# Weight sums of the second feed-forward: two of four made by accumulating transfers, with the signs of the scheme turned

## The chip, the cores and the metric

The kernel runs on one NeuronCore of a Trainium2 chip. The core has five engines with in-order queues of their own: PE (TensorE, matmuls, with its weight loads shown apart as PEld), DVE (VectorE), ACT (ScalarE), POOL (GpSimd) and SP (SyncE, which here only issues DMAs). They work at the same time and wait for each other through semaphores. Sixteen DMA engines move data between the chip's memory (HBM) and the on-chip memory (SBUF); matmul results go to PSUM banks. The metric is the device time of one execution in microseconds (us); the number of record before the change is the median of three runs.

## The reference, cut to what matters

Two layers of a diffusion backbone work on 512 latent tokens of width 1024 (and 256 context tokens). The part that changes is the feed-forward of the second layer, on the latent tokens alone:

```python
def swiglu(h, w_in, w_out):
    gate, up = jnp.split(h @ w_in, 2, axis=-1)
    return (jax.nn.silu(gate) * up) @ w_out

x = x + mx[5] * swiglu(modulate(rms_norm(x, norm2_g[i]), mx[3], mx[4]), ffn_w_in[i], ffn_w_out[i])
```

The inner width is 2816, that is 22 tiles of 128. A tile needs 128 columns of gate weights and 128 columns of up weights, each 1024 deep. All data is 32-bit.

## The kernel before, in words

The weights lie in HBM as one stream `wst` of chunks of 128 x 1024 (512 KB), in the order of their use; SP loads them through `w_raw`. For each FFN tile there are two chunks: `g` (gate) and `u` (up). Their left 512 columns belong to the first half of the model width, their right 512 to the second.

Precision is kept by splitting each operand into a high and a low part, so that one product is three matmuls (high x high, low x high, high x low). The high part is a cast on ACT (line 164, tile `whi`), the low part a subtraction on DVE (line 165, tile `wlo`); both stand in `split`.

Tiles 0, 1 and 2 of the 22 are computed plainly. Tiles 3 to 21 (19 tiles) go through `seven()`: as in Strassen's method the 2 x 2 block product (two halves of the model width, gate and up, two halves of the tokens) is made with seven block products in place of eight. Each product is twelve matmuls of 256 columns (line 897). This needs sums of token blocks, made once (`token_sums`, split into the tiles `sA`), and sums of weight blocks for every tile, made on DVE by `quarter_sums`, lines 903 to 906, each of 128 x 512. With g and u for the left halves g1, u1 and the right halves g2, u2:

- line 903: g1 becomes u1 - g1
- line 904: u1 becomes u2 - u1
- line 905: u2 becomes u2 - (new g1)
- line 906: g2 becomes g2 - (new u2)

Before these sums the old `g` is split whole into `b11`, and the right half of `u` into `b22` (tile `hm`). After them `u` is split into `b32` and `g` into `b14`. The weight pairs b11, b14 and b32 rotate through a ring of six buffers, so a tile's weights can be made while two tiles before it are still multiplied. `g` has two raw buffers of its own in the pool `fp`; `u` shares two raw buffers in the pool `rp` with the weights of the output.

The products go to PSUM tiles X, Y and Z with two banks each. ACT copies four of them to SBUF (lines 1742, 1744, 1746, 1751), DVE adds where two products meet (lines 1748, 1753, 1755), ACT takes the silu (line 107), and DVE multiplies (line 1757). The activation is split in turn (lines 1768, 1770).

The tiles come in groups of 2, 4, 4, 4, 4 and 4. After the first tile of a group the previous group is multiplied by `w_out` (`output`): eight products into the two PSUM banks of `pj`, each added to the residual by DVE (line 256). So PE does four tiles of `seven()`, then an output, and so on.

The order of instructions on each engine is not that of the text: the framework's planner picks it by its own costs and due times, the order of SP's loads included. `after(instruction, others)` adds an order on one engine without a semaphore. POOL has almost nothing to do in this stage. An accumulating DMA, one that adds its source to what stands in its target, is used twice in the kernel before, in the retention layer (line 1466), and is issued from POOL.

Of the kernel before, what the change touches and what calls it, by code (L numbers as in the profile page):

```python
# [30 lines left out]
HALVES = (slice(0, 256), slice(256, 512))  # L31
# [18 lines left out]
def dit_kernel(ctx, tc, xT, cT, crow, small, consts, masks, tabs0, tabs1, jtab, adaQ, adaN, adaT, wst, out):  # L50
    nc = tc.nc
    mult, add, sub = ALU.mult, ALU.add, ALU.subtract
# [9 lines left out]
    def T(pool, cols, tag, bufs, dt=F32):  # L62
        return pool.tile([P, cols], dt, tag=tag, bufs=bufs, name=tag)
# [27 lines left out]
    def after(ins, others):  # L91
        for o in others:
            tc.add_manual_dep(ins.ins, o.ins.name, order, reason="table set turn")
# [24 lines left out]
    wpos, wsel, ring = [0], [0], []  # L118

    def w_raw(pool=None, bufs=2):  # L120
        raw = T(pool or rp, 1024, "wraw", bufs)
        nc.sync.dma_start(raw, wst[wpos[0]])
        wpos[0] += 1
        return raw

    def w_parts(pool, own=2):

        bufs = own
        if ring:
            pool, bufs = ring[wsel[0] % len(ring)], 2  # L130
        elif wsel[0] % (2 + own) < 2:
            pool, bufs = rp, 2
        wsel[0] += 1
        return T(pool, 1024, "whi", bufs, F32R), T(pool, 1024, "wlo", bufs, F32R)
# [28 lines left out]
    def split(t, hi, lo, behind=()):  # L163
        after(nc.scalar.copy(hi, t), behind)  # L164
        return nc.vector.tensor_tensor(lo, t, hi, op=sub)  # L165
# [19 lines left out]
    def t_sq(n):  # L185
        return T(rp, 512, "sq", 2)[:, :n]

    def t_hn(n):
        return T(rp, 512, "hn", 2)[:, :n]
# [609 lines left out]
    t1 = cp.tile([P, 8], F32, name="lg_t1")  # L799
    t2 = cp.tile([P, 8], F32, name="lg_t2")  # L800
# [90 lines left out]
    def product(o, a, b, c0, first):  # L891

        for k in range(4):
            ws = slice(c0 + k * P, c0 + (k + 1) * P)
            (whi, wlo), (xhi, xlo) = (t[:, ws] for t in b), a(k)
            for i, (p, r) in enumerate(((whi, xhi), (wlo, xhi), (whi, xlo))):
                nc.tensor.matmul(o, p, r, start=first and k + i == 0, stop=k == 3 and i == 2,  # L897
                                 skip_group_check=not first)

    def quarter_sums(g, u, behind=()):  # L900

        l_, r_ = slice(0, 512), slice(512, 1024)
        after(nc.vector.tensor_tensor(g[:, l_], u[:, l_], g[:, l_], op=sub), behind)
        nc.vector.tensor_tensor(u[:, l_], u[:, r_], u[:, l_], op=sub)
        nc.vector.tensor_tensor(u[:, r_], u[:, r_], g[:, l_], op=sub)
        nc.vector.tensor_tensor(g[:, r_], g[:, r_], u[:, r_], op=sub)

    for s in range(2):
        fold_gain(0, s, 1)
    F = ExitStack()  # L910
# [40 lines left out]
    def token_sums():  # L951

        h1, h2 = THIRDS
        for k in range(4):
            t1, t2 = tm[k], tm[k + 4]
            for j in (k, k + 4):
                nc.scalar.activation(tm[j][:, h1], tm[j][:, h1], AF.Identity, bias=mods[0, 0][:, 3, j:j + 1])
            nc.vector.tensor_tensor(t2[:, h2], t1[:, h2], t2[:, h2], op=add)
            nc.vector.tensor_tensor(t1[:, h2], t1[:, h1], t1[:, h2], op=sub)
            nc.vector.tensor_tensor(t1[:, h1], t2[:, h2], t1[:, h1], op=sub)  # L960
            nc.vector.tensor_tensor(park[:, k * 384:(k + 1) * 384], t2[:, h1], t1[:, h1], op=sub)
            for n, t in ((1, t2[:, h2]), (3, t1[:, h2]), (2, t1[:, h1])):
                S[n, k] = parts(quarter())
                split(t, *S[n, k])
# [237 lines left out]
    def chunk(i, own=False):  # L1202
        raw = T(qw, 1024, "wx", 4) if own else T(rp, 1024, "wraw", 2)
        nc.sync.dma_start(raw, wst[i])
        return raw
# [6 lines left out]
    last_split, rope_end, rope_sum, hm, other_sums = [None], [None], [None], [], []  # L1212
# [9 lines left out]
            return lambda k: first(4 * (n[1] == "2") + k, int(n[0]) - 1)  # L1222
        return of

    def token_sums(hm, part, sh2, sums, behind=()):

        q1, q2 = HALVES
        shift = mods[1, 0][:, part]
        nc.vector.tensor_tensor(sh2[:, 0:4], shift[:, 0:4], shift[:, 4:8], op=add)
        for k in range(4):  # L1230
            t1, t2 = hm[k], hm[k + 4]
            after(nc.vector.scalar_tensor_tensor(t2[:, q2], t1[:, q2], sh2[:, k:k + 1], t2[:, q2], add, add), behind)
            nc.vector.tensor_tensor(t1[:, q2], t1[:, q1], t1[:, q2], op=sub)
            nc.vector.scalar_tensor_tensor(t1[:, q1], t2[:, q2], shift[:, k:k + 1], t1[:, q1], sub, sub)
            mid = split(t1, *sums[2 * k + 1])
            nc.vector.scalar_tensor_tensor(t2[:, q1], t2[:, q1], shift[:, k + 4:k + 5], t1[:, q1], add, sub)
            other_sums.append((t2, *sums[2 * k]))
        return mid

    def other_parts():  # L1240
        while other_sums:
            split(*other_sums.pop(0))
# [119 lines left out]
    for hd in range(RH):  # L1362
# [20 lines left out]
        if hd == 0:  # L1383
            sums = token_sums(hm, 0, T(qp, 16, "sh2", 1), h_sum, [normed])
            dx, dcx = strips(0, [sums])
# [149 lines left out]
        for i in range(2):  # L1535
            g, v = chunk(bg + i), chunk(bv + i)
# [101 lines left out]
        def first_weights(room, behind=()):  # L1638
            raw = w_raw()
            hi, lo = room()  # L1640
            ahead.append((hi, lo))
            after(nc.scalar.copy(hi, raw), behind)
            return nc.vector.tensor_tensor(lo, raw, hi, op=sub)
# [3 lines left out]
        hm = [T(hM, 512, "hm", 8) for _ in range(KT)]  # L1647
# [26 lines left out]
        for i in (5, 7):  # L1674
            weights_end = first_weights(hW_parts, done[i:i + 1])

    norm_end, first_end, first_mult, first_adds = [], [], [], []
# [15 lines left out]
    sh2 = T(fp, 48, "sh2", 1)  # L1693
    sA = [(T(fp, 512, "sA", 16, F32R), T(fp, 512, "sA", 16, F32R)) for _ in range(KT)]
# [32 lines left out]
    def seven(late=()):  # L1727
        g, u = w_raw(fp, 2), w_raw()
        b11 = w_parts(fp, 4)
        b22 = T(hM, 512, "hm", 8, F32R), T(hM, 512, "hm", 8, F32R)  # L1730
        b14, b32 = w_parts(fp, 4), w_parts(fp, 4)
        split(g, *b11, norm_end)
        split(u[:, 512:1024], *b22, norm_end)
        quarter_sums(g, u, first_end[1:2])
        split(u, *b32, first_adds)
        after(split(g, *b14, first_adds), late)
        X, Y, Z = (T(psF, 512, n, 2)[:, 0:SC] for n in "XYZ")
        t, up = t_hn(SX), t_sq(SX)
        e1, e2 = T(rp, 512, "res", 12), T(rp, 512, "res", 12)
        p1, z1, u2, u3 = e1[:, HALVES[0]], e1[:, HALVES[1]], e2[:, HALVES[0]], e2[:, HALVES[1]]  # L1740
        product(Y, operand_a("11"), b11, 0, True)
        act_parts([nc.scalar.copy(p1, Y)])
        product(Z, operand_a(1), b14, 0, True)
        copies[:] = [nc.scalar.copy(z1, Z)]
        product(Y, operand_a(2), b32, 512, False)
        copies.append(nc.scalar.copy(u2, Y))  # L1746
        product(X, operand_a("12"), b11, 512, True)
        nc.vector.tensor_tensor(t[:, HALVES[0]], p1, X, op=add)
        silu(t[:, HALVES[0]], t[:, HALVES[0]])
        product(Y, operand_a(3), b32, 0, False)  # L1750
        nc.scalar.copy(u3, Y)
        product(Z, operand_a(4), b22, 0, False)
        nc.vector.tensor_tensor(up[:, HALVES[0]], u2, Z, op=add)
        product(Y, operand_a("22"), b14, 512, False)
        nc.vector.tensor_tensor(up[:, HALVES[1]], u3, z1, op=add)
        silu(t[:, HALVES[1]], Y)
        nc.vector.tensor_tensor(t, t, up, op=mult)
        act = new_act()
        pending.append((t, *act))
        return act  # L1760
# [3 lines left out]
    def act_parts(behind=()):  # L1764
        ends = []
        while pending:
            t, hi, lo = pending.pop()
            ends.append(nc.scalar.copy(hi, t))
            after(ends[0], behind)
            ends.append(nc.vector.tensor_tensor(lo, t, hi, op=sub))  # L1770
        return ends
# [24 lines left out]
    for gsz in FFN_GROUPS:  # L1796
        acts = []
        for i in range(gsz):
            if f < 2:
                acts.append(first[f])  # L1800
            elif f == 2:
                w = [next_w(fp, behind=norm_end) for _ in range(2)]
                token_sums(hm, 3, sh2, sA, [weights_end])
                other_parts()
                acts.append(plain(w))
            else:
                acts.append(seven(late))
            late = output(prev, False) if i == 0 and prev is not None else ()
            f += 1
        prev = acts  # L1810
# [146 lines left out]
```

## Time and profile before

| what | value |
|---|---|
| median of 3 runs | 1734.41 us (1733.25 to 1735.33) |
| the profiled execution | 1732.25 us, of which the span of the profile 1730.3 us |
| granted TensorE clock | 0.999 |
| PE busy | 1698.0 us, 98% of the span |
| DVE busy | 1361.0 us, 79% |
| ACT busy | 871.1 us, 50% |
| POOL busy | 50.5 us, 3% |
| first line 903 to last line 906 | 1420.2 us to 1686.5 us |

How to read the rows: in a list of groups, `L164 ACT CAST whi<-wraw` is the line, the engine, the operation, and what it writes and reads; `x19` is a count. In a list of waits, `A <- B: total, times, longest` says that A's engine sat idle until B was done. In the timeline the columns are the start, the duration, and the instruction, with the idle time before it in brackets. In a table of stretches each engine has its busy time and its number of instructions. DMA rows give the size of one transfer in KB and the median time from issue to landing.

### The profile page before, as it was taken

The page shows a single profiled execution, that of the slowest core. Times are in us where ns is not written, and L with a number is a line of the kernel's source. Part 1 is how long each engine was busy: PE and PEld are TensorE (multiplying, and loading weights), DVE is VectorE, ACT ScalarE, POOL GpSimd, SP SyncE. Part 2 cuts the span into 40 slices and gives each one's busy share as a digit, 9 for nine tenths or more (in the row PEclk, how much of TensorE's full clock was granted, in tenths as well). Part 3 has the DMA queues.
Part 4 walks back from the last instruction along what each step waited for, and adds up shares of the span by engine and source line. Part 5 has one row for each costly group of instructions (what it writes and reads, how often), then busy time and mean ns, then how long its engine had stood idle before and what let it go on. Part 6 is the DMA issues. An engine that isn't in the chain of part 4 may idle for free.

```text
span 1730.3 us, 27786 instructions
## 1 busy us (share of the span) xinstructions
PE 1698.0 (98%) x10876; PEld 1513.0 (87%) x10876; DVE 1361.0 (79%) x2436; ACT 871.1 (50%) x1552; POOL 50.5 (3%) x168
## 2 busy tenths in 40 slices
PE   7999999999999999999999999999999999999999
PEld 5788877899999999999988788898897899899998
DVE  6698889798778788787889858858758798877874
ACT  5587779465433334342556534524525464445442
POOL 0000000000000000000000000000000000000000
PEclk9999999999999999999999999999999999999999
DMA  9612221543253434343423524523423223333322
GB/s 349 239 30 57 62 62 56 209 134 121 73 157 117 153 110 148 123 154 102 156 99 88 183 77 132 163 82 124 159 90 108 95 74 103 117 102 116 100 86 86
DMA packets 62803, 207.48 MB, mean 120 GB/s; under 512 B 7248, under 2 KB 8912, under 8 KB 62416
## 3 DMA queue, kind: packets, MB, share of 16 engines
q1 hardware_dynamic: 55184, 178.97, 32.0%
q0 software_dynamic: 7200, 26.22, 5.2%
q8 instruction: 85, 1.39, 0.3%
q10 hardware_dynamic: 288, 0.52, 0.1%
q14 instruction: 46, 0.38, 0.1%
HBM read 199.65 MB, written 2.10 MB: 117 GB/s over the span
## 4 chain that ended last, share of the span: by engine, by line
PE 78%; DVE 11%; DMA 6%; ACT 3%; issue 2%; SPq 0%; ACTq 0%; DVEq 0%
PE Y L897 14%; PE pj L147 7%; PE Z L897 7%; PE pj L149 7%; PE pj L148 7%; PE Z L1292 6%; PE X L897 3%; DMA wraw<-in_wst_dram 3%; PE pT L736 2%; PE pO L750 2%; PE S L710 2%; DVE wlo L165 2%; PE Y L1281 2%; PE pj L1292 2%; PE X L1281 1%
## 5 line engine op out<-in xcount | busy, mean ns | idle before, releaser
L164 ACT CAST whi<-wraw 128x1024 fp32r<-128x1024 f32 x258 | 270.0, 1051 | 333.7 <-PE Z L149 81.9
L165 DVE TENSOR_TENSOR wlo<-wraw,whi 128x1024 fp32r<-128x1024 f32 x258 | 314.3, 1221 | 64.5 <-ACT whi L164 62.7
L897 PE MATMUL Y<-aq,whi 128*128 128x384 f32 x640 | 173.5, 335 | 0.6 <-ACT hn L1053 0.6
L897 PEld LDWEIGHTS Y<-aq,whi 128*128 128x128 f32 x640 | 116.6, 188 | 1.6 <-ACT hn L1053 1.4
L256 DVE SCALAR_TENSOR_TENSOR res<-pj,mod,res 128x512 f32<-128x512 f32 (+1 forms) x112 | 81.0, 728 | 41.5 <-PE pj L149 41.2
L897 PE MATMUL Y<-aq,wlo 128*128 128x384 f32 x320 | 107.0, 334 | 0.0
L273 DVE CUSTOM_DVE_ANT_0 y<-adaw,crow,small_sb 128x1024 bf16<-128x1024 f32 x64 | 81.9, 1280 | 29.6 <-DMA adaw<-in_adaT_dram 29.4
L1292 PE MATMUL Z<-whi,sA 128*128 128x512 f32 x256 | 81.7, 394 | 1.4 <-ACT gate L1478 1.4
L101 ACT ACTIVATE pr<-pr,stat,qs 128x513 f32<-128x513 f32 (+2 forms) x96 | 74.2, 775 | 9.1 <-DVE stat L717 8.8
L147 PE MATMUL pj<-ax,whi 128*128 128x512 f32 x176 | 69.0, 392 | 1.2 <-DVE res L256 1.2
L149 PE MATMUL pj<-ax,whi 128*128 128x512 f32 x176 | 68.6, 390 | 0.0
L148 PE MATMUL pj<-ax,wlo 128*128 128x512 f32 x176 | 68.6, 390 | 0.0
L147 PE MATMUL pj<-act,whi 128*128 128x512 f32 x168 | 65.6, 391 | 0.0
L148 PE MATMUL pj<-act,wlo 128*128 128x512 f32 x168 | 65.5, 390 | 0.0
L149 PE MATMUL pj<-act,whi 128*128 128x512 f32 x168 | 65.5, 391 | 0.0
L897 PEld LDWEIGHTS Y<-aq,wlo 128*128 128x128 f32 x320 | 60.1, 188 | 0.0
L1292 PEld LDWEIGHTS Z<-whi,sA 128*128 128x128 f32 x256 | 48.0, 188 | 13.0 <-ACT gate L1478 2.6
L711 DVE CUSTOM_DVE_ANT_0 pr<-S,mask,qs 128x256 f32<-128x256 f32 (+1 forms) x96 | 53.1, 566 | 7.8 <-PE S L710 5.3
L897 PE MATMUL Y<-sA,whi 128*128 128x256 f32 x304 | 58.1, 277 | 0.6 <-ACT res L1746 0.6
L897 PE MATMUL Y<-hx,whi 128*128 128x256 f32 x304 | 56.3, 277 | 0.0
L736 PE MATMUL pT<-const_sb,pr 128*128 128x128 f32 x352 | 53.6, 278 | 1.5 <-ACT tt L738 0.9
L1292 PE MATMUL Z<-wlo,sA 128*128 128x512 f32 x128 | 50.7, 396 | 0.2
(581 smaller groups left out, 5070.4 us busy)
## 6 DMA issues: line engine op xcount, KB each, us to landing
wraw<-in_wst_dram SPq DMA_DIRECT2D x224, 512.0 KB, 3.6
adaw<-in_adaT_dram POOLq DMA_DIRECT2D x48, 512.0 KB, 3.9
wx<-in_wst_dram SPq DMA_DIRECT2D x30, 512.0 KB, 4.3
adan<-in_adaQ_dram SPq DMA_DIRECT2D x16, 512.0 KB, 8.8
adan<-in_adaN_dram SPq DMA_DIRECT2D x12, 512.0 KB, 7.7
adaw<-in_adaT_dram SPq DMA_DIRECT2D x8, 512.0 KB, 3.9
res<-in_xT_dram SPq DMA_DIRECT2D x14, 256.0 KB, 3.2
aq<-in_adaN_dram SPq DMA_DIRECT2D x12, 256.0 KB, 5.7
```

The costliest lines, as they stand in the source:

```text
L101: ins = nc.scalar.activation(*args, **kw)
L147: nc.tensor.matmul(o, whi, xhi, start=first, stop=False)
L148: nc.tensor.matmul(o, wlo, xhi, start=False, stop=False)
L149: return nc.tensor.matmul(o, whi, xlo, start=False, stop=last)
L164: after(nc.scalar.copy(hi, t), behind)
L165: return nc.vector.tensor_tensor(lo, t, hi, op=sub)
L256: return nc.vector.scalar_tensor_tensor(res[d], o, mods[l, s][:, part, d:d + 1], res[d], mult, add)
L273: res.append(nc.vector.tensor_tensor_reduce(junk, w, cr[:, s * 1024:(s + 1) * 1024], 1.0, sm_t[:, C_ADAB + l * 48 + j:C_ADAB + l * 48 + j ...
L711: nc.vector.tensor_tensor_reduce(pt[:, c0:c0 + w], bank, mask[:, m0:m0 + w], 1.0, top, add, ALU.min, lo)
L736: nc.tensor.transpose(tp[:, a * P:(a + 1) * P], self.pr[(0, 2, 1, 3)[a]][:, ki * P:(ki + 1) * P], ident)
L897: nc.tensor.matmul(o, p, r, start=first and k + i == 0, stop=k == 3 and i == 2, skip_group_check=not first)
L1292: ins = nc.tensor.matmul(os[t], p, r, start=first and k + i == 0, stop=k == 3 and i == 2, skip_group_check=by_k or not first)
```

## The change

In the second feed-forward's `seven()` the four weight sums are replaced by sums without a minus, and the first two of them are made by DMAs that POOL issues and that add to their target in SBUF:

- u1 becomes u1 + u2: an accumulating transfer of 128 x 512 (256 KB) that reads the right half of the same chunk of `wst` from HBM again
- g1 becomes g1 + u1: a second one that reads the left half of u's chunk from HBM
- u2 becomes u2 + (new g1): on DVE, as before, with an addition
- g2 becomes g2 + (new u2): on DVE, as before, with an addition

The second transfer reads `wst`, not the tile `u`, so it doesn't depend on u's load; it does depend on the split of `g` into `b11`, which reads g1 first. To make up for the signs, the token sums swap an addition with a subtraction, and the two sums that form `up` become differences. `token_sums` gets the two operators as an argument; the call in the retention layer keeps the old ones.

```diff
-    def quarter_sums(g, u, behind=()):
-
-        l_, r_ = slice(0, 512), slice(512, 1024)
-        after(nc.vector.tensor_tensor(g[:, l_], u[:, l_], g[:, l_], op=sub), behind)
-        nc.vector.tensor_tensor(u[:, l_], u[:, r_], u[:, l_], op=sub)
-        nc.vector.tensor_tensor(u[:, r_], u[:, r_], g[:, l_], op=sub)
-        nc.vector.tensor_tensor(g[:, r_], g[:, r_], u[:, r_], op=sub)
...
-    def token_sums(hm, part, sh2, sums, behind=()):
+    def token_sums(hm, part, sh2, sums, behind=(), ops=(add, sub)):
...
-        nc.vector.tensor_tensor(sh2[:, 0:4], shift[:, 0:4], shift[:, 4:8], op=add)
+        plus, minus = ops
+        nc.vector.tensor_tensor(sh2[:, 0:4], shift[:, 0:4], shift[:, 4:8], op=plus)
...
-            after(nc.vector.scalar_tensor_tensor(t2[:, q2], t1[:, q2], sh2[:, k:k + 1], t2[:, q2], add, add), behind)
+            after(nc.vector.scalar_tensor_tensor(t2[:, q2], t1[:, q2], sh2[:, k:k + 1], t2[:, q2], add, plus), behind)
...
-            nc.vector.scalar_tensor_tensor(t2[:, q1], t2[:, q1], shift[:, k + 4:k + 5], t1[:, q1], add, sub)
+            nc.vector.scalar_tensor_tensor(t2[:, q1], t2[:, q1], shift[:, k + 4:k + 5], t1[:, q1], add, minus)
...
         split(g, *b11, norm_end)
-        split(u[:, 512:1024], *b22, norm_end)
-        quarter_sums(g, u, first_end[1:2])
+        l_, r_ = slice(0, 512), slice(512, 1024)
+        nc.gpsimd.dma_start(u[:, l_], wst[wpos[0] - 1][:, r_], accum_op=add)
+        split(u[:, r_], *b22, norm_end)
+        nc.gpsimd.dma_start(g[:, l_], wst[wpos[0] - 1][:, l_], accum_op=add)
+        after(nc.vector.tensor_tensor(u[:, r_], u[:, r_], g[:, l_], op=add), first_end[1:2])
+        nc.vector.tensor_tensor(g[:, r_], g[:, r_], u[:, r_], op=add)
         split(u, *b32, first_adds)
         after(split(g, *b14, first_adds), late)
...
-        nc.vector.tensor_tensor(up[:, HALVES[0]], u2, Z, op=add)
+        nc.vector.tensor_tensor(up[:, HALVES[0]], Z, u2, op=sub)
...
-        nc.vector.tensor_tensor(up[:, HALVES[1]], u3, z1, op=add)
+        nc.vector.tensor_tensor(up[:, HALVES[1]], z1, u3, op=sub)
...
-                token_sums(hm, 3, sh2, sA, [weights_end])
+                token_sums(hm, 3, sh2, sA, [weights_end], (sub, add))
```

## The prediction

> **What bounds the kernel now.** I read the engine sums of the page first, then stretches of 50 us over the second feed-forward, because the share of a whole span says little about one stage.
>
> ```profile
> PE 1698.0 (98%) x10876; PEld 1513.0 (87%) x10876; DVE 1361.0 (79%) x2436; ACT 871.1 (50%) x1552; POOL 50.5 (3%) x168
> ```
>
> ```profile
> 1400.00:1450.00 50.00, 48.47 (x370) 45.93 (x370) 48.13 (x75) 27.84 (x45) 0.00 (x0) 1.00 0.27 85
> 1450.00:1500.00 50.00, 49.74 (x338) 45.14 (x337) 37.87 (x53) 22.29 (x38) 0.00 (x0) 1.00 0.40 120
> 1500.00:1550.00 50.00, 50.00 (x371) 47.17 (x370) 38.45 (x54) 24.68 (x43) 0.00 (x0) 1.00 0.33 103
> ...
> 1650.00:1700.00 50.00, 50.00 (x347) 46.25 (x346) 37.33 (x51) 22.86 (x37) 0.00 (x0) 1.00 0.27 85
> ```
>
> The columns after the stretch's length are PE, PEld, DVE, ACT and POOL busy, the granted clock (1.00) and the DMA share. From 1500 us PE has no idle time at all while DVE rests a quarter of the time; only in the first stretch is DVE nearly full (48.13 of 50) and PE idle (1.53 us). Next the waits between 1415 us and the end, as us in total, times, longest:
>
> ```profile
> ACT whi L164 <- DVE wraw L905: 23.3, 18, 2.7
> ...
> PEld pj L147 <- DVE res L256: 2.0, 2, 1.4
> PE pj L147 <- DVE res L256: 1.2, 2, 1.0
> ...
> PEld Y L897 <- ACT res L1746: 0.8, 1, 0.8
> PE Y L897 <- ACT res L1746: 0.6, 1, 0.6
> ```
>
> PE's three waits (2.0 + 0.8 = 2.8 us by the weight loads, 1.2 + 0.6 = 1.8 us by the matmuls) are all that PE loses to DVE and ACT over the 19 tiles that change. ACT does wait for the weight sums (23.3 us), but that is an engine with half its time free.
>
> **What the change removes.** Lines 903 and 904 go; 905 and 906 stay as additions.
>
> ```profile
> L903 DVE TENSOR_TENSOR wraw<-wraw x19: 677/683/694, 1420.2 to 1683.6; 128x512 f32<-128x512 f32 x19
> ```
>
> ```profile
> L904 DVE TENSOR_TENSOR wraw<-wraw x19: 676/683/685, 1421.7 to 1684.5; 128x512 f32<-128x512 f32 x19
> ```
>
> 2 x 19 x 0.683 = 26.0 us of DVE busy time. What covers it is PE, full in every stretch after 1500 us, so there it is worth nothing; it can be worth at most the 2.8 us above, in the early stretch. The turned signs (token sums, lines 1753 and 1755) change operators, not counts or shapes: nothing, since the same instruction stands in the same place.
>
> **What it adds.** 38 accumulating transfers of 256 KB (38 x 256 KB = 10.0 MB more read from HBM), issued from POOL. This kernel already has two of twice the size, at line 1466:
>
> ```profile
> wraw<-in_wst_dram SPq DMA_DIRECT2D x224, 512.0 KB, 3.6
> adaw<-in_adaT_dram POOLq DMA_DIRECT2D x48, 512.0 KB, 3.9
> out_dram<-res SPq DMA_DIRECT2D x8, 256.0 KB, 2.0
> wraw<-in_wst_dram POOLq DMA_DIRECT2D x2, 512.0 KB, 5.7
> ```
>
> ```profile
> L1466 POOL DMA_DIRECT2D wraw<-in_wst_dram x2: 861/872/884, 934.4 to 939.0; - x2
> ...
> DMA to landing us min/median/max: 5.3/5.7/6.1
> ```
>
> The DMA view of 930 to 950 us holds those two and about as many plain bytes, so it prices the engines' time (last column: share of 16 engines):
>
> ```profile
> q0 software_dynamic: 288, 1.05, 32.3%
> q1 hardware_dynamic: 260, 1.01, 15.4%
> ```
>
> An accumulated byte takes twice a plain one: 32.3% of 20 us is 6.5 us on each engine for two transfers, 3.2 us each. Half the size saves half of that, 1.6 us, so I take **T = 5.7 - 1.6 = 4.1 us** from issue to landing. Bounds: 2.0 us (a plain 256 KB store) and 6.1 us (the slower 512 KB accumulate, as if the size saved nothing). 4.1 is nearest the accumulating row, the only one of its kind. The Trainium skill, page "DMA: Bandwidth & Descriptors", section "Anatomy of one DMA — SWDGE (gpsimd) path", fits 2.0 us + bytes/436e3 for a transfer issued from GpSimd, an estimate of 2.6 us for 256 KB and 3.2 us for 512 KB. The row of 512 KB says 5.7 us where the accumulate is done, so here the row decides; with 2.6 us the case below would have 2.5 us to spare instead of 1.0 and the total would be the same.
>
> Engine time added: 38 x 1.6 = 61 us on each DMA engine over some 310 us, which lifts the share from about 0.3 to 0.5; a weight load that meets one lands up to 1.6 us later. POOL issues 38 x 0.87 = 33 us and has nothing else in these stretches (0.00 busy).
>
> **The waits that it adds.** The transfer into u's left half waits for u's load, the one into g's left half for the end of g's first split (line 165). The addition that replaces line 905 waits for g's left half; then DVE and ACT, each in order, hold what is queued behind. One tile in full, whose first product is the second half of the 24 matmuls from 1513.43 below, at 1514.8:
>
> ```profile
> 1502.30 1.23 DVE L165 TENSOR_TENSOR wlo<-wraw,whi 128x1024 fp32r<-128x1024 f32 x1 [0.67 <-ACT whi L164]
> ...
> 1505.43 0.69 DVE L905 TENSOR_TENSOR wraw<-wraw 128x512 f32<-128x512 f32 x1
> ...
> 1509.04 1.22 DVE L165 TENSOR_TENSOR wlo<-wraw,whi 128x1024 fp32r<-128x1024 f32 x1
> ```
>
> ```profile
> 1506.21 1.05 ACT L164 CAST whi<-wraw 128x1024 fp32r<-128x1024 f32 x1 [0.54 <-DVE wraw L905]
> 1507.17 0.36 ACT L1742 COPY res<-Y 128x256 f32<-128x256 f32 x1
> ```
>
> ```profile
> 1510.71 1.36 PE Y L897 x12
> ...
> 1513.43 2.74 PE Y L897 x24
> 1516.17 1.36 PE Z L897 x12
> ```
>
> g's split ends at 1502.30 + 1.23 = 1503.5; the sum lands at 1503.5 + 4.1 = 1507.6, where DVE began line 905 at 1505.43. So the prepared weights come 2.2 us later, the last (b14, the split at 1509.04) at most that: 1510.3 + 2.2 = 1512.5, and PE wants it at 1516.17. Covered, 3.7 us spare. The tighter point is ACT: the cast of b32 (1506.21) moves to 1507.6 + 0.7 = 1508.3, and the copy of line 1742 behind it, which frees a Y bank, ends at 1508.3 + 1.05 + 0.36 = 1509.7. PE needs that bank at 1510.71: 1.0 us spare, and **the limit is T = 5.1 us**. All this keeps the order of the planner, which I can't see for the changed kernel. u's buffer comes free 2.2 us later, and with it the next load, behind which SP holds the others:
>
> ```profile
> 1508.55 0.33 SPq L122 DMA_DIRECT2D wraw<-in_wst_dram  x1
> ```
>
> ```profile
> 1527.38 1.05 ACT L164 CAST whi<-wraw 128x1024 fp32r<-128x1024 f32 x1
> ```
>
> The load issued at 1508.55 takes the 3.6 us of its row and is cast at 1527.38, the next weights of an output: 15 us spare, so zero.
>
> In the output phases DVE also frees the pj banks:
>
> ```profile
> 1539.26 0.69 DVE L903 TENSOR_TENSOR wraw<-wraw 128x512 f32<-128x512 f32 x1 [0.63 <-DMA wraw<-in_wst_dram]
> ...
> 1543.01 0.68 DVE L905 TENSOR_TENSOR wraw<-wraw 128x512 f32<-128x512 f32 x1
> 1543.61 0.74 DVE L256 SCALAR_TENSOR_TENSOR res<-pj,mod,res 128x512 f32<-128x512 f32 x1
> ```
>
> Here line 903 waited for u's load. The new transfer into g reads from HBM what line 903 took from u, so it can start before u lands, if POOL's order lets it; then the sum is there by 1543.01. Zero.
>
> **The early tiles, where something can be won.** The first tile's sums stand before the two L256 for which PE waited most:
>
> ```profile
> 1417.23 1.21 DVE L165 TENSOR_TENSOR wlo<-wraw,whi 128x1024 fp32r<-128x1024 f32 x1
> ...
> 1422.93 0.68 DVE L905 TENSOR_TENSOR wraw<-wraw 128x512 f32<-128x512 f32 x1
> 1423.64 0.69 DVE L906 TENSOR_TENSOR wraw<-wraw 128x512 f32<-128x512 f32 x1
> 1424.25 1.40 DVE L256 SCALAR_TENSOR_TENSOR res<-pj,mod,res 128x512 f32<-128x512 f32 x2
> ```
>
> The sum lands at 1418.4 + 4.1 = 1422.5, before DVE came to line 905, and two instructions that began 0.6 us after one another are gone: L256 comes up to 1.2 us earlier, a gain of 1.2 us, or a loss of 1.6 us if T is 6.1 and the additions stay ahead (1424.5 + 0.7 + 0.7 = 1425.9 against 1424.25); I take the gain. For the Y wait on line 1746 (0.8 us) and the second L256 wait (0.6 us) I take zero: the casts that stand ahead move by less than 1 us, and the sign hangs on the planner's order.
>
> **The sum.** -1.2 us on the profiled execution, 1732.25 us (span 1730.3 and 1.95 around it), gives 1731.0. The median of the runs, 1734.41, is 2.16 us above that execution: 1731.0 + 2.2 = **1733.2 us**, a change of -0.07%. I call 0.2% (3.5 us) about what a measurement here can tell from no change. Best case, all 2.8 us: 1731.6.
>
> **Rivals.**
> - *Slower: engines in order wait on the transfers.* The place is ACT's cast of b32 and DVE's addition ahead of L256; it decides from T = 5.1 us on, or where the planner expects an earlier landing and puts the addition too far ahead. At T = 6.1 a tile as above loses 6.1 - 5.1 = 1.0 us, in some ten of the 19 tiles 10 us, and the first tile 1.6 us: 1734.4 + 11.6 = 1746. If POOL also runs in program order, in the eight or so tiles prepared beside an output the transfer into g waits for u's load (1539.2 + 0.9 + 4.1 = 1544.2 against 1543.01) and L256 behind it is 1.2 us late, up to 10 us more. For it: two transfers of a tile and a load share the same engines, and the 512 KB rows reach 6.1. Against it: the 1.0 us spare at 4.1, and ACT idle in half of its time. I take 1742 as its middle.
> - *Faster by over 0.2%: DVE's 26 us reach the end.* That needs PE to wait for DVE by more than 3.5 us, and the rows hold 2.8 us. As a time, 1729 or less. Only a reordering that I can't see gives it.
> - *The change moves nothing:* the sums were hidden, the transfers are hidden, the early waits stay: 1734.4, within the same bound as my forecast.
>
> **How the numbers follow.** Chances: my forecast together with no movement (1731.6 to 1737.5), 0.53; waits in order, 0.42; faster by over 0.2%, 0.05. The likeliest case's own range is 1731 to 1737.5. The stated range reaches from 1731 to 1748, which leaves out the faster rival and the worst part of the slower one (both additions at full price).
>
> **What would show it.** After the change: L903 and L904 gone and DVE down from 38 to about 34 us busy in each later stretch of 50 us (3.5 tiles x 1.37 = 4.8, less what overlaps); 38 transfers on POOL with a median near 4.1 us; no new PE wait after 1500 us; the L256 wait near 1424 us shorter. I am wrong if PE or PEld shows a wait on ACT L1742 or L1746 or on L256 in each group of tiles, if the median landing is above 5.1 us, or if the addition after the transfer shows a long DVE wait for a DMA with copies late behind it.

## The result and the profile after

The changed kernel takes 1772.36 us (median of 5 runs, 1770.29 to 1773.3) against 1734.41 us before (5 runs, 1733.25 to 1735.88). The ratio is 1.0212, with a 95% interval from 1.0201 to 1.0223: 38 us slower. The profiled execution took 1770.29 us, its span 1768.4 us.

The engine sums of the page of the changed kernel:

```profile
PE 1709.2 (97%) x10876; PEld 1516.7 (86%) x10876; DVE 1339.2 (76%) x2398; ACT 868.6 (49%) x1552; POOL 82.9 (5%) x206
```

DVE's sum fell by 22 us, nearly the 26 us of the removed sums. The span grew all the same. The table of stretches shows the place (after the length: PE, PEld, DVE, ACT and POOL busy, the granted clock, the DMA share):

```profile
1400.00:1450.00 50.00, 46.37 (x340) 43.38 (x339) 42.00 (x68) 24.75 (x40) 4.64 (x6) 0.97 0.43 101
1450.00:1500.00 50.00, 45.60 (x324) 41.64 (x323) 31.74 (x43) 22.67 (x38) 4.72 (x6) 1.00 0.54 136
1500.00:1550.00 50.00, 45.16 (x360) 43.01 (x359) 29.28 (x43) 21.85 (x40) 4.28 (x5) 1.00 0.47 114
...
1650.00:1700.00 50.00, 47.80 (x350) 44.38 (x351) 32.06 (x45) 23.99 (x41) 4.71 (x6) 1.00 0.50 122
```

PE, which had 50.00 of 50 us from 1500 us on, now idles 2 to 5 us in every stretch, while DVE is less busy than before and ACT is busy half of the time or less. So no engine is overloaded: PE waits for something that is late. The waits of the changed kernel between 1415 us and the end (us in total, times, longest) say for what:

```profile
DVE wraw L1730 <- DMA wraw<-in_wst_dram: 43.0, 15, 5.8
ACT whi L164 <- DVE wraw L1730: 34.5, 13, 7.7
...
PEld Y L897 <- ACT res L1743: 18.6, 13, 3.4
...
PEld pj L147 <- DVE res L256: 7.8, 10, 3.1
PEld Y L897 <- ACT res L1739: 7.6, 4, 2.5
```

(Line 1730 is the first addition left on DVE; 1739, 1741, 1743 and 1748 are the copies p1, z1, u2 and u3, which were lines 1742, 1744, 1746 and 1751; 1727 and 1729 issue the transfers into u and g.) PE's three waits are 18.6 + 7.8 + 7.6 = 34.0 us where they were 2.8 us: 31 of the 38 us. The first two rows are the chain behind most of them: the addition waits for the transfer, the casts of b32 and b14 wait for the addition, and on ACT the copies that free bank Y stand behind these casts. Followed back one by one, 12.5 of the 18.6 us at copy u2 and all 7.6 us at p1 stand behind such casts. The other 6.1 us at u2, in three tiles beside an output, stand behind the cast of b22, which waits for a load (shown below).

The landing of the transfers into g, from the view of their line, and the loads and transfers from 1400 to 1765 us in the DMA view:

```profile
L1729 POOL DMA_DIRECT2D wraw<-in_wst_dram x19: 845/855/1197, 1421.3 to 1720.7; - x19
...
DMA to landing us min/median/max: 4.0/5.0/6.7
```

```profile
q1 hardware_dynamic: 9360, 32.25, 28.1%
q0 software_dynamic: 5472, 9.96, 18.3%
...
wraw<-in_wst_dram SPq DMA_DIRECT2D x58, 512.0 KB, 4.0
wraw<-in_wst_dram POOLq DMA_DIRECT2D x38, 256.0 KB, 4.7
```

The 4.1 us of the prediction is the fastest of them, not the middle: 4.7 us is the median over both kinds, 5.0 us that of the transfers into g, on which the additions wait. Loads land in 4.0 us in place of 3.6.

**One steady tile.** In the timeline of the changed kernel (start, duration, instruction, idle time before it), POOL and DVE first, then ACT, then PE:

```profile
1526.63 1.22 DVE L165 TENSOR_TENSOR wlo<-wraw,whi 128x1024 fp32r<-128x1024 f32 x1
...
1528.14 0.85 POOL L1729 DMA_DIRECT2D wraw<-in_wst_dram  x1 [9.36 <-DVE wlo L165]
...
1533.44 0.69 DVE L1730 TENSOR_TENSOR wraw<-wraw 128x512 f32<-128x512 f32 x1 [2.51 <-DMA wraw<-in_wst_dram]
```

```profile
1534.17 1.05 ACT L164 CAST whi<-wraw 128x1024 fp32r<-128x1024 f32 x1 [2.07 <-DVE wraw L1730]
1535.13 0.36 ACT L1741 COPY res<-Z 128x256 f32<-128x256 f32 x1
1535.38 1.04 ACT L164 CAST whi<-wraw 128x1024 fp32r<-128x1024 f32 x1
1536.33 0.37 ACT L1743 COPY res<-Y 128x256 f32<-128x256 f32 x1
```

```profile
1534.97 0.28 PE L897 MATMUL X<-hx,whi 128*128 128x256 f32 x1
1536.76 0.38 PE L897 MATMUL Y<-sA,whi 128*128 128x256 f32 x1 [1.51 <-ACT res L1743]
```

The transfer is issued at 1528.14, when b11's low part is done, and lands 5.3 us later. Then follow, one behind the other, addition, cast of b32, copy z1, cast of b14 and copy u2, which ends at 1536.70. From landing to that end it is 3.3 us, and the same 3.3 us stands in eight more tiles of this trace, all with this order of ACT. PE was done with the product before (X) and could have gone on at 1535.1, 6.9 us after the issue. So in this order of ACT a transfer may take 6.9 - 3.3 = 3.6 us (up to 3.9 us in the other eight tiles, and 2.5 us in the tightest, the third tile). This one took 5.3 us, and PE lost 1.7 us. In the nine tiles together PE's weight loads wait 11.3 us for u2.

**The tile beside an output.** At 1568 us POOL holds a transfer into u of the next tile, which waits for u's load, and behind it the transfer into g of this tile:

```profile
1567.98 0.85 POOL L1727 DMA_DIRECT2D wraw<-in_wst_dram  x1 [8.27 <-DMA wraw<-in_wst_dram]
1568.52 1.20 POOL L1729 DMA_DIRECT2D wraw<-in_wst_dram  x1
```

```profile
1574.95 0.69 DVE L1730 TENSOR_TENSOR wraw<-wraw 128x512 f32<-128x512 f32 x1 [5.49 <-DMA wraw<-in_wst_dram]
```

```profile
1575.81 1.99 ACT L164 CAST whi<-wraw 128x1024 fp32r<-128x1024 f32 x2 [7.74 <-DVE wraw L1730]
1577.70 0.37 ACT L1739 COPY res<-Y 128x256 f32<-128x256 f32 x1
```

The low part that the transfer into g follows ended at 1566.74, so it is issued 1.8 us after it, where a transfer that POOL doesn't hold is issued 0.3 us after. The two transfers run at the same time, the one into g takes 6.4 us, DVE waits 5.5 us, ACT 7.7 us, and the copy p1 behind the two casts frees bank Y so late that PE loses 2.4 us, until 1578.12. ACT had the order of casts and p1 of this tile in the kernel before, too.

The late sum comes back a second time, through u's buffer. SP's next load of u waits until the low part of b32 has read the buffer, and ACT's cast of b22 (tile `hm`) waits for that load, ahead of z1 and u2:

```profile
1576.88 1.22 DVE L165 TENSOR_TENSOR wlo<-wraw,whi 128x1024 fp32r<-128x1024 f32 x1 [0.52 <-ACT whi L164]
...
1578.13 0.33 SPq L122 DMA_DIRECT2D wraw<-in_wst_dram  x1
...
1581.61 0.62 ACT L164 CAST hm<-wraw 128x512 fp32r<-128x512 f32 x1 [3.02 <-DMA wraw<-in_wst_dram]
1582.13 0.37 ACT L1741 COPY res<-Z 128x256 f32<-128x256 f32 x1
1582.40 0.38 ACT L1743 COPY res<-Y 128x256 f32<-128x256 f32 x1
```

The load itself is not slow (3.5 us to landing); it is issued late. PE's weight loads wait 1.9 us for this copy, 6.1 us in the three tiles of this kind.

### The profile page after: what moved, and what is told of

Read it like the earlier page. It is cut to its first block, busy times and chain, and to the rows that moved or that the text cites. A ratio compares the mean times of both kernels' runs of the same rounds, so it can differ in the third digit from the quotient of the medians.

```text
span 1768.4 us, 27909 instructions
## 1 busy us (share of the span) xinstructions
PE 1709.2 (97%) x10876; PEld 1516.7 (86%) x10876; DVE 1339.2 (76%) x2398; ACT 868.6 (49%) x1552; POOL 82.9 (5%) x206
## 4 chain that ended last, share of the span: by engine, by line
PE 63%; DVE 15%; DMA 13%; ACT 4%; issue 4%; SPq 0%; POOL 0%; POOLq 0%; ACTq 0%; DVEq 0%
PE Y L897 10%; DMA wraw<-in_wst_dram 10%; PE pj L147 6%; PE pj L149 6%; PE pj L148 6%; PE Z L897 5%; DVE wlo L165 5%; PE Z L1285 4%; PE pT L736 2%; PE pO L750 2%; ACT whi L164 2%; PE X L897 2%; PE S L710 2%; PE X L1274 1%; PE Y L1274 1%
## 5 line engine op out<-in xcount | busy, mean ns | idle before, releaser
L256 DVE SCALAR_TENSOR_TENSOR res<-pj,mod,res 128x512 f32<-128x512 f32 (+1 forms) x112 | 81.0, 728 | 43.3 <-PE pj L149 42.9
L897 PEld LDWEIGHTS Y<-sA,whi 128*128 128x128 f32 x304 | 49.7, 191 | 26.2 <-ACT res L1743 18.6
```

The lines of the kernel that those rows point to most:

```text
L256: return nc.vector.scalar_tensor_tensor(res[d], o, mods[l, s][:, part, d:d + 1], res[d], mult, add)
```

## The experiments

Theory A: the landing time T of the transfers is too long for the order in which ACT and DVE wait for them, and these hold PE's banks. Rivals: B, the traffic of the transfers slows the loads; C, the turned signs cost something; D, POOL issues in order, so that a transfer into g stands behind another tile's transfer into u; E, ACT's new order costs it whatever T is; F, the cure by order makes the casts too late.

### The signs alone, and the traffic alone

```diff
-        nc.gpsimd.dma_start(u[:, l_], wst[wpos[0] - 1][:, r_], accum_op=add)
...
-        nc.gpsimd.dma_start(g[:, l_], wst[wpos[0] - 1][:, l_], accum_op=add)
-        after(nc.vector.tensor_tensor(u[:, r_], u[:, r_], g[:, l_], op=add), first_end[1:2])
+        after(nc.vector.tensor_tensor(g[:, l_], u[:, l_], g[:, l_], op=add), first_end[1:2])
+        nc.vector.tensor_tensor(u[:, l_], u[:, r_], u[:, l_], op=add)
+        nc.vector.tensor_tensor(u[:, r_], u[:, r_], g[:, l_], op=add)
```

> The turned signs with all four sums of a tile on VectorE and no adding transfer. Theory A (transfers that land late hold ScalarE and VectorE, which run in order, and with them the Y bank and the projection banks of TensorE): with no transfer nothing is late, 1734.4 us as before, within 3.5 us. Theory B (the 38 transfers take DMA time from the weight loads): the same 1734.4. Rival C (the signs themselves, that is the changed token sums, the swapped operands of the two later sums and the shorter chain in u, cost part of it): some of the 37.9 us stays, 1745 us or more.

Measured: 1733.96 us, ratio to before 0.9998 (0.9988 to 1.0007). C is out: the signs are free, and the whole loss comes with the transfers.

To the kernel above, 38 adding transfers into tiles that nobody reads:

```diff
+        nc.vector.tensor_copy(spare[0][:, 0:1], u[:, 0:1])
+        nc.gpsimd.dma_start(spare[0], wst[wpos[0] - 1][:, r_], accum_op=add)
...
+        nc.vector.tensor_copy(spare[1][:, 0:1], b11[1][:, 0:1])
+        nc.gpsimd.dma_start(spare[1], wst[wpos[0] - 1][:, l_], accum_op=add)
```

> All four sums on VectorE with the turned signs, and beside them the same 38 adding transfers of 256 KB, issued at about the same places into two tiles that nobody reads (a copy of one column on VectorE holds each back until the load or the split it follows in the changed kernel). The traffic is that of the changed kernel, nobody waits for it. Theory A: 1734 to 1738 us. Theory B (traffic alone): the loads land later and 10 us or more of the 37.9 show, 1745 to 1772.

Measured: 1741.11 us, ratio 1.0038 (1.0023 to 1.0053), that is 6.5 us (the tiny copies that hold the transfers back are in it). The DMA view of this kernel from 1400 to 1765 us:

```profile
q0 software_dynamic: 5472, 9.96, 17.8%
...
wraw<-in_wst_dram SPq DMA_DIRECT2D x58, 512.0 KB, 3.9
spare<-in_wst_dram POOLq DMA_DIRECT2D x38, 256.0 KB, 5.0
```

The traffic is the same (17.8% against 18.3%), and the transfers are as slow as in the changed kernel. So B explains at most 6.5 us, more than the 0 to 4 us that A had allowed; the other 31 need somebody who waits. The 6.5 us are not all traffic. In the trace the loads ahead of three casts of b22 take 4.5 to 4.8 us where they take 3.6 to 3.8 us with the signs alone, and PE's weight loads wait 3.1 us behind these casts: that is B. Another 2.3 us of PE's wait stand behind a tiny copy that waited for an earlier transfer into its spare tile, and a dip of the granted clock that cost 1.7 us followed (see the last section): that comes at least in part from the way this kernel holds its transfers back.

### Shorter transfers in the same order

```diff
-        nc.gpsimd.dma_start(u[:, l_], wst[wpos[0] - 1][:, r_], accum_op=add)
+        nc.gpsimd.dma_start(u[:, l_], wst[wpos[0] - 1][:, r_])
...
-        nc.gpsimd.dma_start(g[:, l_], wst[wpos[0] - 1][:, l_], accum_op=add)
+        nc.gpsimd.dma_start(g[:, l_], wst[wpos[0] - 1][:, l_])
```

> The changed kernel with its 38 transfers at the same places, of the same size and in the same queue, but overwriting their target in place of adding to it (this leaves the two additions of a tile out, so the sums are other numbers). Every engine's order is that of the changed kernel. Theory A (the landing time T of the transfers sets the loss): loads of 512 KB land in 3.6 to 4.0 us in these traces, so a plain transfer of 256 KB should land in some 2.5 to 3 us in place of 4.7 to 5.0; each of the gaps of 1.2 to 3.5 us shrinks by some 2 us, and the time falls to 1738 to 1750. Rival E (the new order of ScalarE alone costs it, whatever T is) or D (POOL's order, one transfer behind the next tile's load): 1760 or more.

Measured: 1742.39 us, ratio 1.0042 (1.0027 to 1.0057). Every engine issues the same instructions in the same order as in the changed kernel. The landing of the transfers into g in this kernel, from the view of their line, and the queues in its DMA view:

```profile
L1729 POOL DMA_DIRECT2D wraw<-in_wst_dram x19: 536/536/552, 1420.2 to 1695.0; - x19
...
DMA to landing us min/median/max: 2.9/3.4/4.5
```

```profile
q1 hardware_dynamic: 9504, 32.51, 28.4%
...
q0 software_dynamic: 3040, 9.96, 9.1%
```

T fell from 5.0 to 3.4 us, just below the 3.6 us that the steady tile allows, and 30 of the 38 us went. E and D alone are out: the same orders on ACT and on POOL cost 7 us when T is 3.4 us. The tiles agree one by one: the transfer issued at 1518.84 took 3.1 us, and PE lost nothing there.

Half of the columns by transfer, the other half on DVE:

```diff
+        nc.gpsimd.dma_start(u[:, 0:256], wst[wpos[0] - 1][:, 512:768], accum_op=add)
...
+        nc.gpsimd.dma_start(g[:, 0:256], wst[wpos[0] - 1][:, 0:256], accum_op=add)
+        nc.vector.tensor_tensor(g[:, 256:512], u[:, 256:512], g[:, 256:512], op=add)
+        nc.vector.tensor_tensor(u[:, 256:512], u[:, 768:1024], u[:, 256:512], op=add)
```

> Each of the 38 adding transfers carries half its columns (128 KB), and VectorE adds the other 256 columns of the two sums. With T = 4.7 us in the changed kernel the time was 1772, with plain transfers of 3.4 us it was 1742. Theory A (T sets the loss, with a steep part between 3.4 and 5): if T falls with the bytes as the share of DMA time does, about 3 us to landing and 1737 to 1745; if most of T doesn't depend on the size, T stays above 4 and the time above 1755. Rival B (the DMA share): the share of these transfers halves to 9 per cent, like that of the plain ones, and the time is 1742 whatever T is.

Measured: 1742.95 us, ratio 1.0048 (1.0033 to 1.0063). The landing of the transfers into g of 128 KB, in the same view:

```profile
DMA to landing us min/median/max: 3.0/3.5/4.8
```

The same T as plain transfers of twice the size (3.5 and 3.4 us), and the same time. Half the bytes save a good quarter of T, not half, but that was enough. This run does not tell A from B, because both the share and T fell as with the plain transfers; the idle transfers above do, with the full share and only 6.5 us.

### One transfer, and the order on POOL

```diff
-        nc.gpsimd.dma_start(u[:, l_], wst[wpos[0] - 1][:, r_], accum_op=add)
...
+        nc.vector.tensor_tensor(u[:, l_], u[:, r_], u[:, l_], op=add)
```

> Only the transfer into g stays; the sum in u is made by VectorE again. POOL then has one transfer per tile, and none stands behind another that waits for its load. ScalarE's order is that of the changed kernel. Theory A in its plain form (each transfer into g takes 4 to 5 us, and the cast of b32 waits for it in every tile): most of the loss stays, 1764 to 1772 us. Rival D (the loss is that POOL issues in order and the transfer into g stands behind the next tile's transfer into u, and that two transfers in flight slow each other): the gaps at the first tiles of a group go, some 12 to 20 us of them, 1752 to 1760.

Measured: 1754.15 us, ratio 1.0111 (1.0096 to 1.0127); PE, ACT and SP keep the order of the changed kernel. The landing in the view of the transfer's line:

```profile
DMA to landing us min/median/max: 3.9/4.4/5.9
```

Without the second transfer T is 4.4 in place of 5.0 us, and 18 us are back. The plain form of A, which expected no gain here, was wrong to treat T as fixed: two transfers in flight slow each other. In ten tiles of the changed kernel the transfer into u of the next tile runs beside the one into g; there T falls from 5.3 to 4.6 us on average, and in the nine others it stays at 4.6 us. With ACT's order unchanged T = 3.4, 4.4 and 5.0 us go with 1742, 1754 and 1772 us, but the middle point has half the traffic, and nothing on POOL that a transfer into g could stand behind, so it doesn't show the effect of T alone. The next run, which turns only POOL's order, brings back nearly as much.

```diff
+        after(nc.gpsimd.dma_start(u[:, l_], wst[wpos[0] - 1][:, r_], accum_op=add), last_g)
...
+        last_g[:] = [nc.gpsimd.dma_start(g[:, l_], wst[wpos[0] - 1][:, l_], accum_op=add)]
```

> The changed kernel, but POOL issues a tile's transfer into u only behind the transfer into g of the tile before; every other engine keeps its order. Rival D (a transfer into g that is ready stands on POOL behind a transfer into u of a later tile that waits for its load): the gaps of TensorE at the second tiles of the groups (2.4 and 2.0 us at 1576 and 1581, like ones in the other groups, some 12 us in all) go, 1758 to 1762. Theory A in its plain form (landing time alone): 1768 to 1774. If two transfers in flight slow each other, T of the transfer into g falls as well, from 5.0 us towards the 4.4 us that it took alone.

Measured: 1756.03 us, ratio 1.0118 (1.0099 to 1.0137): 16 us back by POOL's order alone, a little more than D expected. Its trace is of the slowest of its four executions (1760.85 us; the fastest took 1753.5 us) and shows 9 us of them. The median T into g falls only to 4.8 us. The clearest effect is the copy p1 (line 1739): PE's weight loads waited 7.6 us for it in the changed kernel and 0.7 us here, because the transfer into g of a tile beside an output no longer waits on POOL for u's load: it is issued at 1564.57, 0.3 us after the low part that it follows, in place of 1.8 us. The four tiles of this kind gain 1.4 to 1.6 us each that way.

### The order on ACT

```diff
-        split(u, *b32, first_adds)
-        after(split(g, *b14, first_adds), late)
+        split(u, *b32, first_adds + copies)
+        after(split(g, *b14, first_adds + copies), late)
```

> The changed kernel with one rule of order more: ScalarE casts b32 and b14 of a tile only behind the copies z1 and u2 of the tile before it, so that these copies, which free banks Z and Y, no longer stand behind a cast that waits for a transfer. The transfers stay as they are. Theory A: the gaps of TensorE at bank Y add up to some 26 us of the 33 in the trace of after, and most of them go, 1772 - 22 = 1750 us (1745 to 1756); what is left are the waits for the projection banks (6 us). Theory B (contention of the transfers with the loads): the loads are as slow as before, 1768 to 1774. Rival F (the casts come too late for their own tile now, 2.2 us later than in after): 1765 or more, with waits of TensorE for b14 and b32 in place of those for bank Y.

Measured: 1753.72 us, ratio 1.0104 (1.0088 to 1.0119), with both transfers kept and T at 5.0 us as in the changed kernel. The casts that wait for the transfers no longer stand ahead of z1 and u2, and half of the loss goes by that alone. What is left has moved, as the waits of this kernel from 1415 us show, and the timeline of one of its tiles:

```profile
PEld Y L897 <- ACT res L1748: 10.6, 9, 2.0
...
PEld pj L147 <- DVE res L256: 8.0, 9, 3.1
```

```profile
1520.79 0.69 DVE L1730 TENSOR_TENSOR wraw<-wraw 128x512 f32<-128x512 f32 x1 [2.46 <-DMA wraw<-in_wst_dram]
...
1522.60 1.23 DVE L165 TENSOR_TENSOR wlo<-wraw,whi 128x1024 fp32r<-128x1024 f32 x1 [0.40 <-ACT whi L164]
1523.74 0.41 DVE L1745 TENSOR_TENSOR hn<-res,X 128x256 f32<-128x256 f32 x1
...
1524.36 0.41 ACT L107 ACTIVATE hn<-hn 128x256 f32<-128x256 f32 x1
1524.68 0.35 ACT L1748 COPY res<-Y 128x256 f32<-128x256 f32 x1
1525.08 0.19 PEld L897 LDWEIGHTS Y<-hx,whi 128*128 128x128 f32 x1 [1.81 <-ACT res L1748]
```

The wait has gone over to DVE: the late addition and the low part behind it hold the addition of X (line 1745), behind that stand the silu and the copy u3 on ACT, and bank Y comes late one product further on. The waits for the pj banks (8.0 us) are what they were.

Three runs combined these cures.

```diff
-        nc.gpsimd.dma_start(u[:, l_], wst[wpos[0] - 1][:, r_], accum_op=add)
...
-        split(u, *b32, first_adds)
+        split(u, *b32, first_adds + copies)
```

> Both earlier cures together: only the transfer into g, and the casts of b32 and b14 behind the copies z1 and u2 of the tile before. Each alone took 18 us of the 38. Theory A with two separate places (the steady tiles, where the cast blocks the copies, and the first tiles of a group, where two transfers queue): the gains add up, 1736 to 1742. Rival (both cures act on the same gaps, and what is left is common to both): 1750 to 1754.

Measured: 1750.64 us, ratio 1.0080 (1.0063 to 1.0096), as the rival had it: the cures do not add.

```diff
-        split(u, *b32, first_adds)
+        split(u, *b32, first_adds + copies)
...
+        after(nc.gpsimd.dma_start(u[:, l_], wst[wpos[0] - 1][:, r_], accum_op=add), last_g)
```

> Both rules of order on the changed kernel, with both transfers at full size: the casts of b32 and b14 behind the copies z1 and u2 of the tile before, and POOL's transfer into u behind the transfer into g of the tile before. Alone they took 18 and 16 us of the 38. If they act on different gaps, 1738 to 1742 us; if on the same ones, as the casts' order and the missing transfer into u did, 1749 to 1754.

Measured: 1752.12 us, ratio 1.0107 (1.0090 to 1.0123). Again hardly better than one of them: PE's waits for p1, which POOL's order takes away, are already gone in the run with the casts behind the copies.

```diff
-        after(nc.vector.tensor_tensor(u[:, r_], u[:, r_], g[:, l_], op=add), first_end[1:2])
+        after(nc.vector.tensor_tensor(u[:, r_], u[:, r_], g[:, l_], op=add), first_end[1:2] + marks[:1])
...
+        split(u, *b32, first_adds + copies + marks[1:])
...
+        marks[:] = [nc.vector.tensor_tensor(t[:, HALVES[0]], p1, X, op=add)]
...
+        marks.append(nc.scalar.copy(u3, Y))
```

> Both transfers kept, and the order turned further than in the run with casts behind copies: the casts also behind the copy u3 of the tile before, and VectorE's first addition of a tile behind the addition of X of the tile before. In that run 10 us of gaps were left at u3 in the second tiles of the groups and 7 us at the projection banks. Theory A: 1740 to 1748. Rival F (the casts come too late for their own tile): 1754 or more, with TensorE waiting for b14 and b32.

Measured: 1755.32 us, ratio 1.0117 (1.0102 to 1.0132). Here the planner also changed PE's order. The waits for bank Y are nearly gone, but PE's weight loads wait 8.5 us for b14's low part (DVE line 165, bank Z): rival F. The three together: with full-size transfers the late sum either holds the banks of the tile before it or comes late for its own tile, and no order tried here had a median below 1750 us.

### An earlier start, and what is left

```diff
-        g, u = w_raw(fp, 2), w_raw()
+        g, u = w_raw(fp, 1), w_raw()
...
-        split(g, *b11, norm_end)
+        g0, g = g, T(fp, 1024, "gsum", 2)
+        nc.sync.dma_start(g, wst[wpos[0] - 2])
+        split(g0, *b11, norm_end)
```

> The changed kernel with g loaded a second time into a tile of its own, to which the transfer adds. The transfer then waits for that load alone and no more for the cast and the low part of b11, which read g; it can start some 3 to 4 us sooner. Price: 19 loads of 512 KB more, and one buffer of g instead of two for the first copy. Theory A: the sums are there before ScalarE comes to the cast of b32, and most of the gaps at bank Y go, but the loads now carry 10 MB more and two transfers a tile besides: 1740 to 1755. Rival B (the DMA share sets it): the loads are late and it becomes slower than the changed kernel, 1772 or more.

Measured: 1769.36 us, ratio 1.0197 (1.0182 to 1.0212). Between the two expectations. The queues of this kernel in the DMA view from 1400 to 1765 us carry much more, and everything in them is later; in ten tiles the transfer into the new tile waits for that tile's load:

```profile
q1 hardware_dynamic: 11978, 41.76, 37.2%
q0 software_dynamic: 5184, 9.44, 16.3%
...
wraw<-in_wst_dram SPq DMA_DIRECT2D x59, 512.0 KB, 4.3
...
gsum<-in_wst_dram POOLq DMA_DIRECT2D x17, 256.0 KB, 5.8
```

It does not tell how much an earlier start would bring by itself, since the one buffer of g and the planner's other order are in it, and so are four dips of the clock behind new gaps, which cost PE 8.5 us in its trace (see the last section).

```diff
+        after(nc.gpsimd.dma_start(u[:, 0:256], wst[wpos[0] - 1][:, 512:768], accum_op=add), last_g)
...
+        last_g[:] = [nc.gpsimd.dma_start(g[:, 0:256], wst[wpos[0] - 1][:, 0:256], accum_op=add)]
```

> Half-size transfers with POOL's order as above. If the 8.6 us that half-size transfers still cost is again landing time and POOL's order, 1736 to 1740; if it is what the traffic costs by itself (6.5 us with transfers that nobody waits for, at full size), it stays at 1740 to 1744.

Measured: 1741.45 us, ratio 1.0040 (1.0025 to 1.0055), the least of all in which a sum waits for a transfer. It lies at the 1741 us of the idle transfers, but that is no proof of a common price of traffic: these transfers carry half the bytes. Its trace has PE's weight loads wait 5.3 us for u2 and 3.6 us for L256, 8.9 us in place of the 2.8 us before, without a clock dip. Of the 5.3 us, 3.5 us stand behind casts that wait for a sum and 1.8 us behind casts of b22 that wait for a load. The waits for L256 are of both kinds, too. So late sums and late loads are both left here, and the runs do not tell what a better order could still save. No version with transfers beats the kernel before: at most 2.8 us could be won, and each of them costs more than that.

## Why the prediction was wrong

The steps in the order of the prediction:

- *PE bounds the kernel, 2.8 us are to be won at most:* right. With DVE unloaded by 22 us nothing was gained anywhere.
- *The turned signs cost nothing:* right (0.9998, 0.9988 to 1.0007).
- *"An accumulated byte takes twice a plain one":* right. For the same 9.96 MB the queue's share is 18.3% with addition and 9.1% without. The forecast of a DMA share of about 0.5 was right too (0.43 to 0.54 in the stretches shown).
- *"T = 5.7 - 1.6 = 4.1 us":* wrong in size. The sum is that of a transfer that meets nothing: the fastest took 4.0 us. In this stage they meet the loads and each other, and the transfers into g took 5.0 us in the median and up to 6.7 us. The prediction's own bounds, 2.0 to 6.1 us, and its remark that a transfer and a load share the engines pointed that way; the middle was taken from a quiet stretch.
- *"the limit is T = 5.1 us":* wrong, and with T this is the step that failed. It stood on "All this keeps the order of the planner". In nine of the 19 tiles the planner moved the cast of b32 from ahead of the copy p1 to ahead of z1 and u2, with the cast of b14 between these two (presumably because it reckons with later sums; no run shows its reasons). In this order the limit is 3.6 us in the steady tile shown, and the nine tiles cost 11.3 us. Even T = 4.1 us would have cost 0.5 us in such a tile. Between the runs with T of 3.4 and 4.4 us, 1742 and 1754 us, a rough estimate for 4.1 us is 1742 + 0.7 x 12 = 1750 us (the second of them differs by more than T): with its own T the prediction would still have been some 17 us short, with the wrong T it was 39 us.
- *A later load has "15 us spare, so zero":* wrong. The load that it priced was one of the next output's. A load of u in the tiles beside an output is needed at once; issued late because u's buffer came free late, it cost PE 6.1 us. That the traffic slows loads was priced at zero too; the idle transfers put that at 6.5 us at most.
- *In the output phases "zero", if POOL's order lets the transfer into g start before u lands:* right for the tile it looked at, wrong for the next. The first tile prepared beside an output had its transfer landed 1.5 to 4.3 us before the addition. For the second POOL's order didn't let it (1567.98 and 1568.52 above), and PE waited 7.6 us at p1; turning that order took back 16 us by the medians.
- *The early tiles win 1.2 us:* wrong in sign. The transfer into g was to start at 1418.4; the low part that it follows ended at 1420.7 in the new order, it was issued at 1421.3 and took 5.5 us, and the L256 behind the additions held PE for up to 3.1 us, the longest wait of the row for pj.
- *The slower rival, "engines in order wait on the transfers":* this is what happened, at both places that it named, ACT's cast of b32 and DVE's addition ahead of L256, and with POOL's order as it feared. It was given 1742 us, at the worst 1746 or 10 us more. It was sized with the 5.1 us of the old order and priced only where T exceeds that; with 3.6 us all nine tiles of the new order pay.

Two of the three signs by which it meant to be shown wrong came true: waits on copies of Y and on L256, and a long DVE wait for a DMA with copies late behind it (43.0 us). The third, a median landing above 5.1 us, did not come (4.7 and 5.0 us), which is one more way to see that the limit had moved.

## What to carry to other kernels

Work moved from an engine with spare time to a DMA trades a duration for a latency: 0.7 us of DVE became 5 us until the data is there, and everything queued behind the waiting instruction on two in-order engines pays for it. Size such a latency from the busiest stretch it will run in, and work out the limit for the order that the planner will choose with the new latency, not for the order in the old trace. Where the engine relieved isn't the bound, only the loss is left.

## What the runs showed of the hardware that was not expected

**Adding transfers and their size.** From issue to landing the fastest adding transfer took 3.0 us for 128 KB and 3.9 us for 256 KB, the fastest of the two of 512 KB in the kernel before 5.3 us; a plain one of 256 KB from the same queue took 2.9 us. A time that doesn't depend on the size, some 2 us by these first two, stays by this estimate whatever is cut. The Trainium skill, page "DMA: Bandwidth & Descriptors", section "Anatomy of one DMA — SWDGE (gpsimd) path", has a fixed part of about 2.0 us too, and its fit gives an estimate of 2.6 us for 256 KB: that is near the 2.9 us of the plain transfer, while the adding one takes 3.9 us at best and 5.0 us among the loads.

**The clock after a pause of PE.** The granted clock fell to half for a moment after some of the new gaps. The table of short stretches of the changed kernel, just behind a gap of 3.05 us between two matmul starts (1426.0 to 1429.1) and one of 2.6 us (1710.8 to 1713.4):

```profile
1430.00:1434.00 4.00, 4.00 (x13) 3.13 (x12) 3.04 (x5) 1.57 (x2) 0.00 (x0) 0.57 0.00 0
...
1713.00:1717.00 4.00, 3.58 (x17) 3.59 (x18) 3.46 (x5) 1.53 (x5) 0.00 (x0) 0.57 0.41 131
```

A mean of 0.57 over 4 us is 3.4 us at half clock, or 1.7 us lost each time, 3.4 us of the 38. With the 31 us of waits that places 35 us; the rest was not located. The other four executions had a mean clock of 0.993 to 0.995, against 0.996 here, so they may hold more such dips. Over all kernels run here, 20 gaps between matmul starts after 1400 us were longer than 2.2 us, and 12 of them were followed by such a dip; one of 2.28 us was, one of 3.52 us was not. One more dip, in the kernel of rival F, came behind two gaps of 0.4 and 1.8 us in a row. The Trainium skill, page "TensorE: Matmul & The Clock Gate", section "Part 1: The HAM clock gate (the "warmup" mystery)", describes a free-running window of about 3.4 us and a half-rate clock after an idle window. The length of the dips agrees and so does that the same gap may or may not be followed by one; that a single pause well below 3.4 us can be enough is what these runs add.
